# Depthwise taps on TensorE as phases, a modulation on VectorE, and more of a down projection as block products

## The chip, the cores and the metric

The kernel runs on one core of a Trainium2 chip. The metric is the device time of one execution in microseconds (us). The engines are TensorE (PE in the profile), VectorE (DVE), ScalarE (ACT), GpSimd (POOL) and SyncE (SP), whose queue issues most of the DMAs; POOL issues the rest, among them DMAs that add to what lies at their destination.

## The reference

Two layers of a residual trunk on a sequence of 1024 tokens with 1024 channels, all in float32. In both layers:

```
mod = silu(c) @ ada_w[i] + ada_b[i]
sh_m, sc_m, g_m, sh_f, sc_f, g_f = split(mod, 6)          # columns 0 to 5 of the modulation
h = rms_norm(x) * (1 + sc_m) + sh_m
y = conformer_conv(h) in layer 0, multiscale_pool(h) in layer 1
x = x + (1 + g_m) * y
h = rms_norm(x) * (1 + sc_f) + sh_f
x = x + (1 + g_f) * ((silu(h @ w_gate) * (h @ w_up)) @ w_down)      # F = 2816
```

The convolution module of layer 0 is a product to 2048 columns with a gate (GLU), a causal depthwise convolution of width 31 (each channel has 31 taps of its own over the sequence), a layer norm over channels, a silu and a product to 1024. A last RMSNorm ends the stack.

## The kernel before

Channels lie on the 128 partitions, in 8 channel tiles; the sequence is cut into two halves (chunks A and B of 512 tokens). A product in float32 is made of three products of rounded parts: the high part of the weight with the high and with the low part of the activation, and the low part of the weight with the high one (`products`, line 517). So each block of 128 x 128 weights costs three products of 512 columns, and each weight is split into two parts after it has landed, by ScalarE and VectorE (a *direct* weight), or by two passes of ScalarE and a DMA from POOL that adds the weight to its negated high part (a *summed* weight, `load_weight`, line 493).

PE's order is written out by hand: the program is a list of units, each with the weights that it takes, and `run_units` loads the weights ahead in five buffers (`W_BUFS`), with three buffers for raw blocks. The other engines' instructions are ordered by a planner that simulates them. Work of VectorE and POOL that has no fixed place (taps, norms, modulation dots) is kept in tasks, and `pace` lets them step as far as the clocks of a cost model allow (`Engine`, `PRICES`); `finish` forces tasks to their end before the units behind it are written.

Layer 0 starts with the GLU of each channel tile (`conv_in`, `conv_glu`). Two tiles of chunk A get help from PE for their taps: `PE_TAPS = {6: 15, 7: CW}`. A tap on PE is a product with a diagonal block that holds the tap's 128 weights; there are 46 such blocks, in 6 units of up to 8. All other taps are done by VectorE (`ca` in the profile) or by ScalarE and POOL together (`pr` and `pa`), a scaled and shifted add of 512 columns each; the class `Taps` holds them. The order around it: conv of chunk B's tiles 6 and 7 (in one unit with chunk A's), then of tiles 0 and 1, then the units of `pe_taps`, then `finish` of all taps of chunk A, then conv of chunk B's tiles 2, 3 and 4 while chunk A's layer norm (`layer_norm_silu`) runs, then chunk A's product to 1024 (`conv_out`, tile `y`), then tile 5 of chunk B behind which the feed-forward norm of chunk A (`norm_a`) is made.

Columns 2 and 3 of layer 0's modulation, and then 4 and 5, come from PE (`ada_columns`: products of 32 x 256 with c, four side by side, tiles `ada` and `adac`); layer 1's come from VectorE as dots of 1024 columns (`ada_task`).

The feed-forward of layer 0 works on 11 pairs of F tiles. For the pairs from `BEGINS[0] = 8` on, the gate's results are combined over the two halves and the tiles of a pair into seven kinds (`paired` in `joint`), which go to DRAM, and the down projection of those pairs is made of seven block products instead of eight (steps p1 to p7 in `first_down`). The other pairs go the plain way: even tiles of chunk A in `down` between the first heads, odd ones of chunk A in steps a and b, and chunk B's in steps c to f. Each combined step takes a pair of weight tiles and a pair of operand tiles that are split on the way. Chunk A is whole after p4; layer 1's pooling of chunk A (`pool`) then runs beside the rest, and its products (`pool_out`, tile `mx`) stand after step e.

Of the kernel before, what the change touches and what calls it, by code (L numbers as in the profile page):

```python
# [52 lines left out]
PE_TAPS = {6: 15, 7: CW}  # L53
# [7 lines left out]
BEGINS = (8, 0)  # L61
# [38 lines left out]


def tap_groups(p):

    n = PE_TAPS[p]

    todo = list(range(CW - 1, -1, -1) if n == CW else range(CW - 3, CW - 3 - 2 * n, -2))
    return [todo[i : i + DIAGS] for i in range(0, len(todo), DIAGS)]
# [26 lines left out]
def trunk(ctx, tc, xT, c, vec, ada, adan, w1f, w1, wdg, w2, wgu, wdn, wds, wpl, out):  # L134
# [210 lines left out]
    kinds_d = [{q: [dram.tile([P, 2, 2, 512], F32, name=f"kinds_{l}_{q}_{b}") for b in range(3)] for q in BY_SEVEN[l]} for l in range(DEPTH)]  # L345
    KINDS = {"t1": (0, 0), "b22": (0, 1), "t3": (1, 0), "t2": (1, 1), "b11": (2, 0), "t4": (2, 1)}
# [55 lines left out]
    def ada_task(l, js, pause=None, first=None):  # L402

        def gen():
            todo = [(j, k) for j in js for k in range(KT)]
            ws = [ada_load(ada[(l * 6 + j) * KT + k], soft) for j, k in todo[:ADA_BUFS]]
            for i, (j, k) in enumerate(todo):
                yield first if first and i == 0 else pause or ("next" if "pooled" in st else "slow")
                ada_dot(ws.pop(0), l, j, k)
                if i + ADA_BUFS < len(todo):  # L410
                    j2, k2 = todo[i + ADA_BUFS]
                    ws.append(ada_load(ada[(l * 6 + j2) * KT + k2], soft))
# [327 lines left out]
    def conv_glu(ch, p, ba, bg, own=False):  # L740
        u = st["u", ch.i, p]
# [4 lines left out]
        if ch.i == 0 and PE_TAPS.get(p) == CW:  # L746

            V_.scalar_tensor_tensor(ba, ba, V("conv_b1", p), sg, op0=ADD, op1=MUL)
            pair = wpair(B, "us", F32R)
            hi, lo = st["us", p] = [pair[:, i, : ch.width] for i in range(2)]  # L750
            for part in (hi, lo):
                G_.memset(part[:, HALO - 2 : HALO].bitcast(F32), 0.0)
            S_.copy(hi[:, HALO:], ba)
            V_.tensor_tensor(lo[:, HALO:], ba, hi[:, HALO:].bitcast(F32), op=SUB)
            S_.copy(uhalo[:, p, :], ba[:, ch.n - HALO :])
            return
# [6 lines left out]
    def conv_in(*todo, fine=4):  # L763

        def emit(take):
            got = {}
            for each in todo:
# [4 lines left out]
                conv_u(ch, p)  # L772
# [10 lines left out]
                if ch.i == 0 and PE_TAPS.get(p, 0) < CW:  # L783
                    T["taps", 0, p] = Taps(A, p)
                if ch.i == 0 and p == KT - 1:
                    for q in PE_TAPS:
                        if PE_TAPS[q] < CW:
                            split_u(q)
# [3 lines left out]
    def split_u(p):  # L792

        u = st["u", 0, p][:, HALO - 2 : HALO - 2 + A.n]
        hi, lo = st["us", p] = pair("h0", "us")
        S_.copy(hi, u)
        either(A.n).tensor_tensor(lo, u, hi.bitcast(F32), op=SUB)

    def pe_taps(p):


        groups = tap_groups(p)
        us = []
        for i, js in enumerate(groups):
            def emit(take, i=i, js=js):
                if i == 0:
                    st["tap", p] = bank("tap")
                b, wt = st["tap", p], take()
                for q, j in enumerate(js):
                    full = PE_TAPS[p] == CW  # L810
                    o = (CW - 1 - j) // 2 * 2 if full else CW - 3 - j
                    c = j + o if full else 0
                    products(b[:, o:], wt, q, [v[:, c : c + A.n - o] for v in st["us", p]], j == groups[0][0], j == groups[-1][-1])
                    if q % 4 == 3:
                        pace()
                if i == len(groups) - 1:
                    if full:
                        S_.activation(st["u", 0, p][:, HALO:], b, AF.Identity, bias=V("conv_bdw", p))
# [1201 lines left out]
    for p in rest[: len(rest) - HOLD - HOLD_LN]:  # L2020
        conv_in((B, p))
# [235 lines left out]
```

## Time and profile before

| | us |
|---|---|
| median of 3 runs | 1676.87 (1676.09 to 1678.81) |
| profiled execution, its own time | 1675.66 |
| its span from the first to the last instruction | 1673.9 |
| PE busy | 1651.8 |
| VectorE busy | 1310.0 |
| ScalarE busy | 804.1 |
| POOL busy | 487.4 |

An engine is busy while it executes; the span less the busy time is its idle time. The granted TensorE clock was 0.998. The chain of work that ended last, followed back from the last instruction, is 88% products of PE. L128 and L151 are lines of helpers through which all vector instructions and all products are written, so groups are told apart by the tile written and the tiles read (`tap<-us,w`).

### The profile page before, as it was taken

What the parts mean: (1) busy time and instruction counts of PE and PEld (TensorE: products, weight loads), DVE (VectorE), ACT (ScalarE), POOL (GpSimd) and SP (SyncE); (2) the same over time, 40 slices, a digit from 0 to 9 for tenths busy, and PEclk for the clock granted to TensorE, in tenths of its full rate; (3) what the DMA queues carried; (4) which work ended last, traced back from release to release, by engine and by line L of the source; (5) the groups of instructions that cost most, each with busy time, mean ns of one, the idle gap of its engine ahead of it and who ended that gap; (6) DMA issues with size and microseconds to landing.
All of it is one profiled execution on the core that took longest, in us unless ns stands there. A gap on an engine that the chain in (4) does not pass through costs nothing.

```text
span 1673.9 us, 21194 instructions
## 1 busy us (share of the span) xinstructions
PE 1651.8 (99%) x7550; PEld 1351.2 (81%) x7550; DVE 1310.0 (78%) x1867; ACT 804.1 (48%) x1090; POOL 487.4 (29%) x567
## 2 busy tenths in 40 slices
PE   7999999999999999999999999999999999999997
PEld 5777878787888888888888888888888888888887
DVE  8889899799759888888678957848777766658657
ACT  3669696867546332332234436637322222244354
POOL 3587777796002111221100502101111111000013
PEclk9999999999999999999999999999999999999999
DMA  8958997828776888886965959866777776686664
GB/s 301 295 176 228 225 236 205 226 78 241 229 234 168 278 264 287 282 272 206 400 231 164 285 155 283 247 211 199 189 225 222 220 227 183 207 273 207 192 170 126
DMA packets 117180, 378.60 MB, mean 226 GB/s; under 512 B 12369, under 2 KB 14545, under 8 KB 117074
## 3 DMA queue, kind: packets, MB, share of 16 engines
q1 hardware_dynamic: 79664, 245.63, 41.6%
q0 software_dynamic: 36832, 131.09, 32.5%
q8 instruction: 59, 0.97, 0.2%
q10 hardware_dynamic: 578, 0.53, 0.1%
q14 instruction: 47, 0.39, 0.1%
HBM read 310.61 MB, written 62.39 MB: 223 GB/s over the span
## 4 chain that ended last, share of the span: by engine, by line
PE 88%; POOL 3%; DVE 2%; DMA 2%; issue 2%; ACT 2%; DVEq 0%; SPq 0%; POOLq 0%; ACTq 0%
PE a L151 24%; PE dn L151 23%; PE e L151 14%; PE p L151 10%; PE y L151 6%; POOL pa L128 3%; PE first L151 3%; PE g L151 2%; PE tap L151 2%; DMA adaw<-in_adan_dram 1%; DMA s<-in_wds_dram 1%; PE ada L151 1%; ACT w L128 1%; DMA w<-in_wgu_dram 1%; PE var L151 1%
## 5 line engine op out<-in xcount | busy, mean ns | idle before, releaser
L128 ACT CAST w<-raw 128x1024 fp32r<-128x1024 f32 (+1 forms) x247 | 254.6, 1033 | 305.5 <-PE dn L151 56.9
L128 DVE TENSOR_TENSOR w<-raw,w 128x1024 fp32r<-128x1024 f32 (+1 forms) x173 | 209.3, 1214 | 62.2 <-ACT w L128 61.9
L151 PE MATMUL a<-n,w 128*128 128x512 f32 x1056 | 246.8, 389 | 0.2
L151 PE MATMUL p<-h,w 128*128 128x512 f32 x1056 | 243.7, 390 | 1.2 <-DMA w<-in_wgu_dram 1.0
L128 POOL TENSOR_TENSOR pa<-pa,pr 128x512 f32<-128x512 f32 x159 | 225.3, 1500 | 29.0 <-ACT pr L128 23.7
L151 PEld LDWEIGHTS p<-h,w 128*128 128x128 f32 x1056 | 197.3, 188 | 43.7 <-DMA w<-in_wgu_dram 1.4
L151 PEld LDWEIGHTS a<-n,w 128*128 128x128 f32 x1056 | 198.0, 188 | 42.2 <-DVE r L128 1.1
L151 PE MATMUL dn<-hi,w 128*128 128x512 f32 (+1 forms) x768 | 226.2, 377 | 0.4 <-DVE w L128 0.4
L151 PE MATMUL dn<-g,w 128*128 128x512 f32 x864 | 199.1, 390 | 0.2 <-DVE x L128 0.2
L151 PEld LDWEIGHTS dn<-g,w 128*128 128x128 f32 x864 | 161.7, 188 | 34.7 <-DVE x L128 0.6
L128 DVE SCALAR_TENSOR_TENSOR ca<-u,vecs,ca 128x512 f32<-128x512 f32 x246 | 170.6, 747 | 0.5
L151 PEld LDWEIGHTS dn<-hi,w 128*128 128x128 f32 x768 | 141.2, 188 | 27.0 <-DVE w L128 0.9
L151 PE MATMUL dn<-lo,w 128*128 128x512 f32 (+1 forms) x384 | 144.3, 376 | 0.0
L151 PE MATMUL a<-t,w 128*128 128x512 f32 x528 | 123.3, 389 | 0.0
L151 PE MATMUL e<-t,w 128*128 128x512 f32 x528 | 123.3, 389 | 0.0
L151 PE MATMUL e<-b,w 128*128 128x512 f32 x528 | 123.3, 389 | 0.0
L128 ACT ACTIVATE pr<-u,vecs 128x512 f32<-128x512 f32 x159 | 108.4, 717 | 25.0 <-POOL pa L128 19.7
L151 PEld LDWEIGHTS a<-t,w 128*128 128x128 f32 x528 | 99.1, 188 | 20.7
L151 PEld LDWEIGHTS e<-t,w 128*128 128x128 f32 x528 | 99.1, 188 | 20.6
L151 PEld LDWEIGHTS e<-b,w 128*128 128x128 f32 x528 | 99.1, 188 | 20.6
L1191 POOL DMA_DIRECT2D raw<-in_wgu_dram x41 | 36.5, 889 | 271.5 <-DVE r L128 104.2
L128 ACT CAST hi<-op 128x1024 fp32r<-128x1024 f32 (+1 forms) x52 | 48.5, 935 | 87.1 <-PE dn L151 77.2
(191 smaller groups left out, 2449.4 us busy)
## 6 DMA issues: line engine op xcount, KB each, us to landing
raw<-in_wgu_dram SPq DMA_DIRECT2D x132, 512.0 KB, 4.7
raw<-in_wds_dram SPq DMA_DIRECT2D x48, 512.0 KB, 6.0
adaw<-in_ada_dram POOLq DMA_DIRECT2D x48, 512.0 KB, 6.8
kinds<-k POOLq DMA_DIRECT2D x42, 512.0 KB, 7.7
raw<-in_wgu_dram POOLq DMA_DIRECT2D x41, 512.0 KB, 7.3
raw<-in_w_dram SPq DMA_DIRECT2D x36, 512.0 KB, 6.6
op<-kinds SPq DMA_DIRECT2D x36, 512.0 KB, 4.8
adaw<-in_adan_dram SPq DMA_DIRECT2D x32, 512.0 KB, 5.5
```

The source lines that it names most:

```text
L128: self.last = self.order(getattr(self.eng, name)(out, *args, **kw))
L151: last_mm[0] = nc.tensor.matmul(out, lhsT, rhs, start=start, stop=stop, skip_group_check=more).ins.name
L1191: d = order(nc.gpsimd.dma_start(w[i], wgu[l, fp, src], accum_op=ADD))
```

## The change

Three parts.

**Taps of channel tiles 6 and 7.** All 31 taps of both tiles go to PE, for both chunks. After the GLU the values of a tile are written to DRAM by phases (token modulo 4) and read back with 32 channels x 4 phases on the partitions, for each of four groups of 32 channels. Along the partitions a product then sums over four neighbouring tokens, and nine blocks of weights, each shifted by one column of four tokens, hold all taps. For each tile, 4 groups x 9 blocks, with three products of 256 columns each (both chunks at once), in 9 units of 8 blocks; every other one of these weights is direct. ScalarE copies the results out, they go to DRAM and come back by channels, and ScalarE adds the bias into `u` (`tapped`). The units of taps now stand behind the conv of chunk B's tile 0, and its tile 1 behind them. Chunk B's tiles 6 and 7 have no taps left on the other engines, nor has chunk A's tile 6.

**Columns 4 and 5 of layer 0's modulation** come from VectorE as dots, with loads on SP's queue.

**Layer 0's down projection**: `BEGINS[0]` is 6 instead of 8, so pairs 6 to 10 (F tiles 12 to 21) are made by seven block products. The even tiles of pairs 6 and 7 keep only half of their plain products for chunk A between the heads; p2 leaves pairs 6 and 7 out. Steps a and b have three units instead of four, the steps of chunk B run over three quads of tiles, the blocks a22 are loaded where they are used, four low parts of one quad's operands are made by POOL, and the pooled products stand after step d.

```diff
-PE_TAPS = {6: 15, 7: CW}
+ON_PE = (6, 7)
+PHASES = 4
+GC = P // PHASES
+NM = (CW - 1 + 2 * (PHASES - 1)) // PHASES
+LEAD = NM - 1
+SEG = 2 * WSLOT // PHASES
...
-BEGINS = (8, 0)
+BEGINS = (6, 0)
...
+    def phased(ch, p, ba, sg):
+        n = ch.n // PHASES
+        t = temp(ch.n, "ny", 2)
+        V_.scalar_tensor_tensor(t.rearrange("p (f n) -> p f n", f=PHASES), ba.rearrange("p (n f) -> p f n", f=PHASES), V("conv_b1", p),
+                                sg.rearrange("p (n f) -> p f n", f=PHASES), op0=ADD, op1=MUL)
+        d = phased_d[p][ch.i]
+        sync.dma_start(d.rearrange("p f n -> p (f n)"), t)
+        if ch.i == 0:
+            st["us", p] = phase_parts(p)
+        o = LEAD + ch.i * n
+        view = d.rearrange("(g c) f n -> f c g n", c=GC)
+        for gs, hi, lo in st["us", p]:
+            for f in range(PHASES):
+                sync.dma_start(lo[GC * f : GC * f + GC, : len(gs), o : o + n].bitcast(F32), view[f][:, gs[0] : gs[-1] + 1])
+            at = (slice(None), slice(0, len(gs)), slice(o, o + n))
+            S_.copy(hi[at], lo[at].bitcast(F32))
+            V_.tensor_tensor(lo[at], lo[at].bitcast(F32), hi[at].bitcast(F32), op=SUB)
...
+    def pe_taps():
+        blocks = [(p, g, m) for p in ON_PE for g in range(PHASES) for m in range(NM)]
+        n = S // PHASES
...
+                    products(b[:, g % 2 * n : g % 2 * n + n], wt, q, (hi, lo), m == 0, m == NM - 1, more=True)
...
+                    if m == NM - 1 and g % 2:
+                        out_ = temp(2 * n, "acc", 2)
+                        S_.copy(out_, b)
+                        sync.dma_start(tapped_d[p][:, g - 1 : g + 1], out_.rearrange("p (g n) -> p g n", g=2))
+                        if g == PHASES - 1:
+                            tapped(A, p)
...
+        for i in range(0, len(blocks), DIAGS):
+            units_.append((emit_of(blocks[i : i + DIAGS]), wdg[i // DIAGS] if i // DIAGS % 2 else direct(wdg[i // DIAGS])))
...
+    def tapped(ch, p):
...
+        t = temp(ch.n, "ny", 2).rearrange("p (f n) -> p f n", f=PHASES)
+        view = tapped_d[p].rearrange("(f c) g n -> g c f n", f=PHASES)
+        for g in range(PHASES):
+            sync.dma_start(t[GC * g : GC * g + GC], view[g][:, :, ch.i * n : ch.i * n + n])
+        S_.activation(u[:, HALO:].rearrange("p (n f) -> p n f", f=PHASES), t.rearrange("p f n -> p n f"), AF.Identity, bias=V("conv_bdw", p))
+        st["taps", ch.i][p] = True
...
-                gs = [st["g", ch.i, f] for f in fs]
+                gs = [st["g", ch.i, f] for f in fs if not d0 or f // 2 < BEGINS[l]]
...
-            V_.tensor_tensor(lo[:, :w], raw[:, :w], hi[:, :w].bitcast(F32), op=SUB)
+            eng = G_ if not l and q == 3 and kind in ("b11", "t2", "t3", "t4") else V_
+            eng.tensor_tensor(lo[:, :w], raw[:, :w], hi[:, :w].bitcast(F32), op=SUB)
...
+            at_once = {"a12": 1, "s4": 1, "a22": 3, "s2": 3}.get(kind)
+            if at_once is not None:
+                mine["a22" if kind == "s2" else kind] = r = raws.tile([P, D], F32, tag="raw", name=nm("raw"))[:, :n]
+                nc.sync.dma_start(r, wds[l, q, at_once][:, :n])
...
+            mine = [q for q in qs if kind != "a12" or q >= ROUNDS[l] * ROUND // 2]
...
-        classical(A, range(duo), 0, ("odd",), "a")
-        classical(A, range(duo), 1, ("odd",), "b")
+        classical(A, range(begins), 0, ("odd",), "a")
+        classical(A, range(begins), 1, ("odd",), "b")
...
-        for qs, names in ((range(duo // 2), "cd"), (range(duo // 2, duo), "ef")):
+        for some_qs, names in ((range(2), "cd"), (range(2, begins), "ef")):
...
-    for p in rest[: len(rest) - HOLD - HOLD_LN]:
+    first, *others = rest[: len(rest) - HOLD - HOLD_LN]
+    conv_in((B, first))
+    for u in pe_taps():
+        unit(*u)
+    for p in others:
         conv_in((B, p))
-    for p in PE_TAPS:
-        for u in pe_taps(p):
-            unit(*u)
+    unit(lambda take: [tapped(B, p) for p in ON_PE])
...
-        T["ada_f"] = Task(ada_columns((4, 5)), False, 0)
-        T["ada_f"].free = True
+        T["ada_f"] = ada_task(0, (4, 5), queue=sync)
     unit(ada_second)
-    taps(B, *some, *rest[: len(rest) - HOLD - HOLD_LN])
+    taps(B, *rest[: len(rest) - HOLD - HOLD_LN])
...
-        "e": lambda: pool_end(A),
+        "d": lambda: pool_end(A),
```

More of the change, by code (lines that the diff above doesn't have):

```diff
@@ L745, in conv_glu @@
             tc.add_manual_dep(S_.last.ins, st.pop("v_high"), edge, reason="behind the layer norm's last high part")
[L746 to L755, printed above, removed]
+        if p in ON_PE:
+            phased(ch, p, ba, sg)
             return
@@ L799, in pe_taps, with phase_parts @@
[L799 to L813, printed above, removed]
+    def phase_parts(p):
+        if p == ON_PE[0]:
+            hi, lo = (wpair(B, "us", F32R).rearrange("p a (b w) -> p (a b) w", w=SEG) for _ in range(2))
+            parts = [(range(PHASES), hi, lo)]
+        else:
+            parts = [(range(o, o + 2), block("h0", "us"), block("h0", "us")) for o in range(0, PHASES, 2)]
+        for _, hi, lo in parts:
+            for part in (hi, lo):
+                G_.memset(part[:, :, :LEAD].bitcast(F32), 0.0)
+        return parts
@@ new lines, in pe_taps, with emit_of, emit @@
+    def pe_taps():
+        blocks = [(p, g, m) for p in ON_PE for g in range(PHASES) for m in range(NM)]
+        n = S // PHASES
+        units_ = []
+        def emit_of(these):
+            def emit(take):
+                wt = take()
+                for q, (p, g, m) in enumerate(these):
+                    if m == 0 and g % 2 == 0:
+                        st["tap"] = bank("tap")
+                    b = st["tap"]
+                    hi, lo = next((hi[:, g - gs[0], m : m + n], lo[:, g - gs[0], m : m + n]) for gs, hi, lo in st["us", p] if g in gs)
+                    products(b[:, g % 2 * n : g % 2 * n + n], wt, q, (hi, lo), m == 0, m == NM - 1, more=True)
@@ L832, in __init__ @@
             self.ch, self.p, self.done, self.urgent = ch, p, False, False
-            self.acc, self.part, self.other = None, None, None
-            others = tap_groups(p) if ch.i == 0 and p in PE_TAPS else []
-            self.todo, self.awaits = [j for j in range(CW - 1) if not any(j in js for js in others)], bool(others)
+            self.acc, self.part = None, None
+            self.todo = list(range(CW - 1))
             tasks.append(self)
@@ L1655, in first_down @@
         SIDE = {"odd": 0, "even": 1}
-        duo, one = BY_SEVEN[l]
-        todo, raw, banks, ready, counts = [], {duo: {}, one: {}}, {}, {}, [0, 0]
+        qs = list(BY_SEVEN[l])[::-1]
+        begins = BEGINS[l] // 2
+        raw, banks, ready, counts = {q: {} for q in qs}, {}, {}, [0, 0]
         steps = []
```

114 lines of the change are left out of this document (47 added, 67 removed).

## The prediction

> **What bounds the kernel now.** I read the first two parts of the page, then who made TensorE (PE) wait, then the busy time by stage.
>
> ```profile
> span 1673.9 us, 21194 instructions
> PE 1651.8 (99%) x7550; PEld 1351.2 (81%) x7550; DVE 1310.0 (78%) x1867; ACT 804.1 (48%) x1090; POOL 487.4 (29%) x567
> PE   7999999999999999999999999999999999999997
> ...
> PE p L151 <- DMA w<-in_wgu_dram: 1.0, 1, 1.0
> ...
> 66.00:167.00 101.00, 100.71 (x523) 75.21 (x522) 91.50 (x144) 83.18 (x121) 79.49 (x75) 1.00 0.75 215
> 167.00:200.00 33.00, 33.00 (x159) 26.67 (x152) 31.05 (x48) 22.80 (x30) 29.16 (x27) 1.00 0.89 220
> 200.00:245.00 45.00, 44.95 (x236) 34.77 (x235) 38.01 (x64) 37.18 (x50) 27.76 (x27) 1.00 0.95 240
> ...
> 816.00:860.00 44.00, 44.00 (x196) 36.44 (x195) 24.60 (x34) 9.71 (x12) 3.79 (x7) 1.00 0.93 350
> 860.00:918.00 58.00, 58.00 (x264) 48.17 (x263) 51.20 (x73) 26.69 (x35) 3.30 (x12) 1.00 0.52 153
> ```
>
> A window row gives its length and then the busy time of PE, weight loads, VectorE (DVE), ScalarE (ACT) and POOL; its last numbers are clock, DMA share and GB/s. The 22.1 us that PE is idle lie almost all in the first and the last slice. Between them its longest wait is 1.0 us, and in the stages that the change touches (167 to 245 us, 816 to 918 us) it has next to none. So the order of products written for PE sets the time: a product taken out is worth its issue time, unless one of the others, which must now deliver sooner, comes too late.
>
> **The price of a product.** A product's "mean ns" overlaps its neighbours, so I take the time of runs in the chain of waits (start, length, what).
>
> ```profile
> 167.38 5.69 PE tap L151 x24
> 173.64 7.68 PE tap L151 x33
> 181.66 18.47 PE tap L151 x81
> ...
> 516.73 5.44 PE e L151 x24
> ...
> 1650.24 6.47 PE dn L151 x54
> ...
> L151 PE MATMUL dn<-hi,w 128*128 128x256 f32 x36 | 6.7, 285 | 0.0
> L151 PEld LDWEIGHTS dn<-hi,w 128*128 128x128 f32 x35 | 5.5, 191 | 0.0
> ```
>
> 512 columns: 5.44 / 24 = 0.227 us. 256 columns, as in the last stage: 6.47 / 54 = 0.120 us, each with a weight load of its own (the last two rows, window 1650.3 to 1656.7 us). I take 0.120.
>
> **Taps.** Removed: 15 taps of tile 6 and 31 of tile 7, three products each, 138; they take 5.69 + 7.68 + 18.47 = 31.8 us. Added: 2 tiles x 4 output groups x 9 blocks x 3 products of 256 columns = 216, for both halves of the sequence: 216 x 0.120 = 25.9 us. PE: **-5.9 us**. If the short products ran at half the 512 price, 0.114, it would be -7.2; if each took the 0.191 of its weight load, +9.5. VectorE and POOL lose 62 taps of the second half and 16 of the first, and two closing sums.
>
> The Trainium skill (TensorE: Matmul & The Clock Gate, Part 3, "What overlaps and what doesn't") says that weight loads overlap running matmuls only where their row groups differ; all of these use the whole array, so by it each load would stand in series. By that rule the change would lose at this place; the row above (0.120 us with a 191 ns load) goes against it, and I give it a small chance below.
>
> **Modulation.** Columns 4 and 5 of the modulation leave PE:
>
> ```profile
> 211.84 1.07 PE L151 MATMUL ada<-adaw,ccols 128*32 128x256 f32 x16
> 212.84 5.78 PE L151 MATMUL a<-h,w 128*128 128x512 f32 x24
> ...
> 267.91 0.50 PE L151 MATMUL adac<-quarters,t 128*128 128x4 f32 x4
> 268.27 11.13 PE L151 MATMUL y<-v,w 128*128 128x512 f32 x48
> ...
> 317.56 1.07 PE L151 MATMUL ada<-adaw,ccols 128*32 128x256 f32 x16
> ...
> 921.02 1.22 DVE L128 SCALAR_TENSOR_TENSOR adaw<-adaw,cact 128x1024 f32<-128x1024 f32 x1
> ```
>
> Eight such pairs stand between the first row and the last of its kind, 1.00 us each (212.84 - 211.84), and two turns of 0.36 (268.27 - 267.91): **-8.7 us**. VectorE gets 16 dots of 1.22 us, 19.5 us over some 100 us, less than half of the 62 taps that it and POOL no longer do (0.66 us each on VectorE, 9.30 / 14 in the row under step 2: 41 us); the same 512 KB per dot is loaded on the same queue (SP). The dots are paced 6 us apart; column 4 needs eight, 48 us, and comes before the 336 products ahead of it (76 us) have passed, so its forced finish costs nothing. If that cover were gone, each dot left over would be 1.2 us of wait for the feed-forward norm.
>
> **Down.** Pairs 6 and 7 took 2 x 96 = 192 products in the plain form (2 tiles x 2 halves x 8 x 3 a pair) and take 2 x 84 = 168 as seven blocks: 24 fewer of 0.227, **-5.4 us**. Their kind sums replace splits of the same size on VectorE, under joint units for which PE waited nowhere.
>
> Together -20.0 us on PE. Now what is late next.
>
> **1. The feed of the tap weights.** A unit is 24 products, 24 x 0.120 = 2.9 us, where it was 5.7.
>
> ```profile
> raw<-in_wdg_dram SPq DMA_DIRECT2D x6, 512.0 KB, 6.9
> w<-in_wdg_dram POOLq DMA_DIRECT2D x6, 512.0 KB, 9.3
> ...
> L128 ACT CAST w<-raw 128x1024 fp32r<-128x1024 f32 (+1 forms) x247 | 254.6, 1033 | 305.5 <-PE dn L151 56.9
> L128 DVE TENSOR_TENSOR w<-raw,w 128x1024 fp32r<-128x1024 f32 (+1 forms) x173 | 209.3, 1214 | 62.2 <-ACT w L128 61.9
> L506 POOL DMA_DIRECT2D w<-in_wdg_dram x6 | 7.0, 1165 | 4.3 <-ACT t L128 2.8 <-ACT w L128 1.6
> ```
>
> Five weight buffers: a buffer freed by one unit is needed four units later, 11.5 us. A summed weight takes two ACT passes (2.1), the issue (1.2) and 9.3 us of landing, 12.6 us; a direct one, with its raw block already there, 1.0 + 1.2 = 2.2 us. Four of nine are summed, and two of those fill a buffer inside the run: 2 x 1.1, I take **+2 us**. Bounds: nothing, if the landing is the 6.9 of the other queue; +7 if SP is held up once by a pair of the new writes (rival b). SP carries eight writes to DRAM here, with reads that wait at the head of the queue until they have landed, and the raw weights queue behind those. The nearest write-and-read-back is that of the kind sums:
>
> ```profile
> kinds<-k POOLq DMA_DIRECT2D x42, 512.0 KB, 7.7
> op<-kinds SPq DMA_DIRECT2D x36, 512.0 KB, 4.8
> ```
>
> The way there and back is 7.7 + 4.8 = 12.5 us. Between the last product of tile 6's second half and its first tap product lie 96 others (21.8 us: tile 7 and one conv tile more); tile 7's have 48 and the 108 tap products of tile 6 (10.9 + 13.0 = 23.9 us). Both cover the way, by 9 us.
>
> **2. Layer norm of the first half.** All its taps must be in before its mean.
>
> ```profile
> 170.75 9.30 DVE L128 SCALAR_TENSOR_TENSOR ca<-u,vecs,ca 128x512 f32<-128x512 f32 x14
> ...
> 203.35 1.50 DVE L128 TENSOR_TENSOR acc<-acc,u 128x512 f32<-128x512 f32 x2
> 205.43 1.02 PE L151 MATMUL mean<-acc,ones 128*128 128x512 f32 x2
> 221.41 6.01 DVE L128 SCALAR_TENSOR_TENSOR ca<-u,vecs,ca 128x512 f32<-128x512 f32 x9
> ...
> 238.91 11.58 PE L151 MATMUL y<-v,w 128*128 128x512 f32 x48
> ...
> 241.92 0.69 DVE L128 TENSOR_TENSOR v<-t,v 128x512 fp32r<-128x512 f32 x1 [1.11 <-ACT v L128]
> ...
> L128 DVE SCALAR_TENSOR_TENSOR ca<-u,vecs,ca 128x512 f32<-128x512 f32 x118 | 81.9, 748 | 0.4
> L128 POOL TENSOR_TENSOR pa<-pa,pr 128x512 f32<-128x512 f32 x65 | 92.6, 1566 | 8.0 <-ACT pr L128 4.2 <-ACT uhalo L128 3.1
> ```
>
> The sum is ready at 204.85 and the mean runs at 205.43: 0.6 us of room. PE will be there 5.9 us sooner. By the last two rows (window 66 to 205.5 us) VectorE did about 63% of the taps. So 16 taps and their closing give back some 8.7 us on VectorE and 8.4 on POOL, and two fewer summed weights 2.3 on POOL. Five direct tap weights (5 x 1.2) and two more splits take 7 us of VectorE. What is left, 1.7 us of VectorE (0.66 a tap) and 10.7 of POOL (92.6 / 65 = 1.42 a tap), is 10.1 taps; both engines together do 2.22 taps in a us, so the sum is ready 4.5 us sooner: 0.8 us late. From mean to y three modulation pairs fall out (3.0 us); the last low part ends at 242.6 and is read at 238.91 + 7 x 0.68 = 243.7, 1.1 us of room: 1.9 us late. Together **+2.7 us**. Bounds: 0, if the fillers between its steps move aside (6 us of other taps stand there); 8.8 if nothing of it gets sooner. The path from the last tap product through ACT, DRAM and ACT again (one cast, 12.5 us by the rows, one scatter) ends near 195, some 14 us behind the last product, ahead of the vector taps.
>
> **3. First down.** The classical part ahead of the blocks (a, b) shrinks from 8 units to 6, 43.5 to 32.6 us, and "d" takes the place of "e" as the point where the pooling must be done:
>
> ```profile
> 964.30 0.68 DVE L128 TENSOR_TENSOR mx<-win,mx 128x512 fp32r<-128x512 f32 x1
> ...
> 983.47 11.04 PE L151 MATMUL y<-mx,w 128*128 128x512 f32 x48
> ```
>
> It ends at 965.0 for products at 983.5, 18.5 us of room. From the end of p4 to these products there were 72 products of p5 and p3 (16.3 us) and 288 of c, d, e (65.3); there will be 120 (27.2) and 192 (43.5), 10.9 us less, which leaves 7.6. VectorE had 51.2 of 58 us busy in the old blocks, but a step of two pairs is 5.4 us of products for 2.4 of splits, and four splits go to POOL, which had 3.3. The loads are nearer: 350 GB/s over 44 us is 15.4 MB; less two weights (1.0 MB) it takes 41 us in a window of 33, 8 us late if all of it were wanted by the first block. Most is not, so I take **+1.5 us**, between 0 and 8.
>
> **Sum.** 1675.7 (the profiled execution, 1673.9 of span and 1.8 around it) - 20.0 + 2 + 2.7 + 1.5 = 1661.9. The median of the runs is 1.2 us above that execution: **1663 us**, 0.8% faster.
>
> **Rivals.** (a) *The waits eat half.* Layer norm and first down take their upper bounds, 8.8 + 8, in place of 4.2: 1676 us, within 0.2%; with one of them 1669. For it: the 0.6 and 1.1 us of room. Against it: VectorE and POOL lose 78 taps. (b) *SP's queue becomes the bound, and it is slower.* The writes come in pairs (two output copies of a tile, two halves of its values). If both hold the head of SP for 7.7 us, 15.4 us stand against the three raw blocks loaded ahead, 3 x 2.9 = 8.7: PE waits 6.7 us. Four pairs make 26.8: 1676.9 - 20.0 + 26.8 = 1684 us. It is slower than before once a hold costs over 6.9 us (2 x 6.9 - 8.7 = 5.0, four times 20). For it: the DMA share of 0.89 to 0.95 there. Against it: a write is 256 KB, not 512, and the first two pairs fall under conv products, where a weight lasts 5.4 us and not 2.9. (c) *Weight loads don't hide* behind 256 columns: 216 x (0.191 + 0.120) = 67.2 us, +35.4 on the old taps: 1676.9 + 35.4 - 14.1 = 1698. Against it stands the 0.120. (d) *Nothing is late*: 1657.
>
> **How the numbers follow.** Forecast 0.58, (d) 0.12, (a) 0.17 (a third of it near 1676), (b) 0.10, (c) 0.03. A change under 0.2% (3.4 us) can't be told from none. Faster: 0.58 + 0.12 + 0.11 = 0.81; within 0.2%: 0.06 of (a) and 0.01 of (b), 0.07; slower 0.12. The range runs from 1655 (d with 0.114 us a product) to 1677, the far end of (a); (b) and (c) lie outside.
>
> **What would show it.** Right: 216 tap products at 0.12 us in about 26 us; no modulation products after the taps; 24 fewer down products; PE busy near 1632 us and its idle time 22 + 6. Wrong: PE waiting in the taps for weights over 4 us (step 1), for the mean or y over 5 (step 2), in p2 to p6 or ahead of the pooled y (step 3). A rate of 0.15 us or more would upset the first term; a wait of PE for the tap values themselves, the cover of the round trip.

## The result and the profile after

The changed kernel takes 1736.12 us (median, 1732.8 to 1739.1) where the kernel before, on the same chip, takes 1677.62: a ratio of 1.0349, 95% interval 1.0328 to 1.037. It is 3.5% slower; the forecast was 1663 us, and no rival reached this far. The profiled execution took 1736.28. One execution of an experiment below (2063.7 us, at a granted clock of 0.75) fell in a slower state of the chip and is left out of that experiment's median.

The first lines of the page of the kernel after:

```profile
span 1734.4 us, 21107 instructions
PE 1650.5 (95%) x7468; PEld 1353.3 (78%) x7468; DVE 1330.2 (77%) x1848; ACT 804.3 (46%) x1086; POOL 491.5 (28%) x556
...
PEclk9999999799999999999999999999999999999999
```

PE is idle for 83.9 us (1734.4 - 1650.5) where it was 22.1. And it is busy for as long as before, though 20 us of products are gone: the clock row has a dip, and products are slower there. The span's growth is then -20.0 (products) + 61.8 (idle) + 18.7 (what is left of busy time: 1650.5 - 1651.8 + 20.0) = 60.5 us. By stage, the first answer is the kernel before, the second the kernel after (columns as in the prediction, where the first row of the kernel before stands, 66 to 167 us). The stages are: up to the first tap product; to the first product of the feed-forward; to `y` of the second half; to the blocks of the first down; to the pooled `y`; the rest.

```profile
167.00:300.00 133.00, 132.95 (x677) 105.17 (x670) 120.72 (x194) 99.31 (x135) 100.31 (x90) 1.00 0.87 223
300.00:450.00 150.00, 148.49 (x680) 119.84 (x679) 133.78 (x189) 109.62 (x161) 95.67 (x74) 1.00 0.61 181
450.00:860.00 410.00, 409.89 (x1815) 339.19 (x1814) 316.85 (x437) 146.69 (x194) 68.95 (x112) 1.00 0.84 270
860.00:984.00 124.00, 124.00 (x555) 102.83 (x554) 101.08 (x146) 54.07 (x69) 25.81 (x48) 1.00 0.69 209
984.00:1674.00 690.00, 681.10 (x3103) 566.88 (x3101) 489.53 (x671) 284.46 (x380) 93.02 (x124) 1.00 0.70 208
```

```profile
66.00:155.00 89.00, 88.18 (x454) 66.22 (x452) 79.99 (x119) 72.01 (x107) 65.77 (x60) 1.00 0.74 212
155.00:326.00 171.00, 138.54 (x721) 115.74 (x719) 133.08 (x201) 115.56 (x158) 112.34 (x98) 0.90 0.79 209
326.00:497.00 171.00, 148.91 (x617) 119.00 (x618) 138.72 (x184) 107.40 (x155) 93.37 (x69) 0.93 0.63 195
497.00:896.00 399.00, 398.89 (x1767) 330.08 (x1766) 310.23 (x429) 137.97 (x180) 68.17 (x111) 1.00 0.82 262
896.00:1044.00 148.00, 140.34 (x605) 113.93 (x604) 122.56 (x160) 60.27 (x75) 38.80 (x52) 0.98 0.63 198
1044.00:1734.00 690.00, 681.35 (x3102) 566.94 (x3101) 489.15 (x669) 284.75 (x380) 88.91 (x121) 0.99 0.68 206
```

The first stage is 12 us shorter, and the fourth and fifth trade some 11, only because units stand elsewhere in PE's order (48 conv products behind the first tap, 48 down products behind the first block). The loss lies in three stages: 38 us, less those 12, around the taps and the first norms, 21 up to the second half's `y`, and 24, less those 11, in the blocks. The last 690 us are the same to the microsecond. The five largest waits of PE after (in total, times, longest):

```profile
PE mean L148 <- DVE acc L125: 21.8, 2, 12.4
PE p L148 <- ACT h L125: 15.1, 1, 15.1
PE p L148 <- ACT r L125: 8.2, 2, 7.1
PE var L148 <- DVE acc L125: 8.1, 2, 6.0
PE dn L148 <- DVE x L125: 4.3, 4, 2.1
```

**Place 1, the mean of the first half (12.4 us).** PE's rows, then ScalarE's, then those of SP's queue (in brackets the idle time before a row and what ended it; L148 and L125 are the helpers' lines here that were L151 and L128 before):

```profile
160.04 8.60 PE L148 MATMUL tap<-us,w 128*128 128x256 f32 x47 [3.91 <-DMA raw<-in_wdg_dram]
...
169.14 5.99 PE L148 MATMUL tap<-us,w 128*128 128x256 f32 x48
...
189.70 1.67 PE L148 MATMUL tap<-us,w 128*128 128x256 f32 x12
...
220.12 2.05 PE L148 MATMUL mean<-acc,ones 128*128 128x512 f32 x2 [12.37 <-DVE acc L125]
```

```profile
194.58 0.56 ACT L125 COPY acc<-tap 128x512 f32<-128x512 f32 x1
...
210.81 1.17 ACT L125 ACTIVATE u<-ny,vecs 128x512 f32<-128x512 f32 x1 [10.63 <-DMA ny<-tapped]
211.88 0.67 ACT L125 ACTIVATE t<-g,vecs 128x512 f32<-128x512 f32 x1
...
218.08 2.26 ACT L125 ACTIVATE u<-ny,vecs 128x512 f32<-128x512 f32 x2
```

```profile
196.24 0.43 SPq L166 DMA_DIRECT2D tapped<-acc  x1
196.72 1.97 SPq L166 DMA_DIRECT2D ny<-tapped  x4
201.99 2.55 SPq L495 DMA_DIRECT2D raw<-in_w_dram  x2
209.28 4.45 SPq L166 DMA_DIRECT2D ny<-tapped  x6
```

```profile
SPq L166 <- DMA tapped<-acc: 13.2, 4, 4.7
```

The last tap product ends at 191.4, its result is copied at 194.6, written to DRAM from 196.2, read from 209.3 on and scattered at 218.1: 27 us where the prediction had 14. The last row (of SP's waits) shows SP at the head of its queue for that write, which landed at 209.2, 13.0 us after its issue. Meanwhile ScalarE stands 10.6 us at a scatter whose values have not come. It is not the one that the mean needs: it belongs to the second half's tile 6, whose four reads went out at 196.7, while the first half's last two went out only at 209.3. Behind it in ScalarE's queue stands the sigmoid of the next conv tile (`t<-g`), for which VectorE then waits 10.1 us; VectorE's own sums end at 218.1, the one with the scattered values at 220.0.

**Place 2, the feed-forward norm (15.1 us).** PE, then VectorE:

```profile
325.81 0.80 PE L148 MATMUL p<-h,w 128*128 128x512 f32 x1 [15.13 <-ACT h L125]
```

```profile
304.56 2.21 DVE L125 SCALAR_TENSOR_TENSOR adaw<-adaw,cact 128x1024 f32<-128x1024 f32 x1
...
322.07 1.23 DVE L125 SCALAR_TENSOR_TENSOR adaw<-adaw,cact 128x1024 f32<-128x1024 f32 x1 [2.45 <-DMA adaw<-in_ada_dram]
...
324.25 1.40 DVE L125 SCALAR_TENSOR_TENSOR t<-x,gains,rstd 128x512 f32<-128x512 f32 x2 [0.94 <-POOL gains L125]
```

Six dots run between the norm's root (done at 304.6) and the first value of the norm, which needs column 4 from them. They were not late: `mean_rsqrt` puts the last six dots (`recent`, `RECENT = 6`) behind the root, so that they don't delay it. Here the norm itself wants the column. Their loads run only two ahead, so three of the six also waited for a load, 9.1 us together.

**Place 3** is the second half's layer norm (9.4 us ahead of its mean, 7.1 behind it), **place 4** the blocks of the first down. The 6.0 us ahead of a `var` are none of the change's places: they lie at 11.9 us, where the kernel before waits 4.9.

### The profile page after: what moved, and what is told of

Its sections match the earlier page's. It is cut to its first block, busy times and chain, and to the rows that moved or that the text cites. A ratio compares the mean times of both kernels' runs of the same rounds, so it can differ in the third digit from the quotient of the medians.

```text
span 1734.4 us, 21107 instructions
## 1 busy us (share of the span) xinstructions
PE 1650.5 (95%) x7468; PEld 1353.3 (78%) x7468; DVE 1330.2 (77%) x1848; ACT 804.3 (46%) x1086; POOL 491.5 (28%) x556
## 5 line engine op out<-in xcount | busy, mean ns | idle before, releaser
L125 ACT CAST w<-raw 128x1024 fp32r<-128x1024 f32 (+1 forms) x242 | 250.0, 1036 | 282.1 <-DMA raw<-in_wgu_dram 56.6
L148 PE MATMUL p<-h,w 128*128 128x512 f32 x1056 | 251.2, 398 | 24.2 <-ACT h L125 15.1
L148 PE MATMUL dn<-hi,w 128*128 128x512 f32 (+1 forms) x864 | 259.4, 381 | 6.1 <-DVE x L125 4.0
L148 PEld LDWEIGHTS p<-h,w 128*128 128x128 f32 x1056 | 202.4, 193 | 69.1 <-ACT h L125 15.5
L125 DVE TENSOR_TENSOR w<-raw,w 128x1024 fp32r<-128x1024 f32 (+1 forms) x172 | 217.3, 1268 | 41.4 <-ACT w L125 41.3
L148 PE MATMUL a<-n,w 128*128 128x512 f32 x1056 | 246.8, 389 | 0.2
L148 PEld LDWEIGHTS a<-n,w 128*128 128x128 f32 x1056 | 198.1, 188 | 42.1 <-DVE r L125 1.1
L125 POOL TENSOR_TENSOR pa<-pa,pr 128x512 f32<-128x512 f32 x148 | 218.8, 1528 | 41.4 <-ACT pr L125 38.0
L148 PEld LDWEIGHTS dn<-hi,w 128*128 128x128 f32 x864 | 160.8, 190 | 39.5 <-DVE x L125 3.4
L148 PE MATMUL dn<-g,w 128*128 128x512 f32 x696 | 161.3, 391 | 3.5 <-DVE g L125 2.5
L148 PE MATMUL dn<-lo,w 128*128 128x512 f32 (+1 forms) x432 | 164.4, 381 | 0.0
L148 PEld LDWEIGHTS dn<-g,w 128*128 128x128 f32 x696 | 130.0, 188 | 32.9 <-DVE g L125 3.7
L125 DVE SCALAR_TENSOR_TENSOR ca<-u,vecs,ca 128x512 f32<-128x512 f32 x188 | 130.3, 746 | 0.2
L148 PE MATMUL a<-t,w 128*128 128x512 f32 x528 | 123.3, 389 | 0.0
L148 PE MATMUL e<-t,w 128*128 128x512 f32 x528 | 123.2, 389 | 0.0
L148 PE MATMUL e<-b,w 128*128 128x512 f32 x528 | 123.2, 389 | 0.0
L148 PEld LDWEIGHTS a<-t,w 128*128 128x128 f32 x528 | 99.1, 188 | 20.7
L148 PEld LDWEIGHTS e<-t,w 128*128 128x128 f32 x528 | 99.1, 188 | 20.6
L148 PEld LDWEIGHTS e<-b,w 128*128 128x128 f32 x528 | 99.1, 188 | 20.6
L125 DVE SCALAR_TENSOR_TENSOR adaw<-adaw,cact 128x1024 f32<-128x1024 f32 x80 | 104.8, 1315 | 10.3 <-DMA adaw<-in_ada_dram 10.3
L125 ACT ACTIVATE pr<-u,vecs 128x512 f32<-128x512 f32 x148 | 100.9, 716 | 22.9 <-POOL pa L125 15.4
```

The lines of the kernel that those rows point to most:

```text
L125: self.last = self.order(getattr(self.eng, name)(out, *args, **kw))
L148: last_mm[0] = nc.tensor.matmul(out, lhsT, rhs, start=start, stop=stop, skip_group_check=more).ins.name
```

## The experiments

The time of the kernel before in these comparisons was 1676.5 to 1677.6 us. "Offset" is how much later than before a point in PE's row comes.

### Each part alone

The diff is cut into its three parts and each is put alone on the kernel before.

> The kernel before with the first part alone (taps of tiles 6 and 7 as phases). Theory 1 (each part brings a wait of its own; here the way of the tap results back through DRAM, 27 us from the last tap product to the vector sum instead of the 14 that was reckoned): a wait of PE for the first layer norm's mean of 8 to 14 us, products at a lower granted clock behind it, 1685 to 1700 us. Rival (the three parts only hurt together, because they share the DMA queues and VectorE): no wait over 3 us, about 1672 us.

> The kernel before with the second part alone (columns 4 and 5 of the first layer's modulation as dots on VectorE). Theory 1 (six dots of column 4 are ordered behind the root of the very norm that needs them, by the list of the last six dots that the norm puts behind its root): six dots between the root and the first scaled value, a wait of PE for h of 10 to 16 us at the first heads, 1680 to 1695 us. Rival (dots are only late because the taps' transfers hold up their loads): column 4 done before the root, about 1669 us.

> The kernel before with the third part alone (five pairs by seven block products). Theory 1: some 7 to 8 us of idle time of PE between the first block products and the pooling, 1676 to 1684 us. Rival (its waits come from the stages ahead of it): no idle time there, 1672 us.

Measured: taps 1692.73 us (ratio 1.0089, 1.0072 to 1.0106), modulation 1712.42 (1.021, 1.0195 to 1.0226), down 1697.59 (1.0118, 1.0103 to 1.0133). Each part alone is slower. +15.7, +35.4 and +20.6 make 71.7, more than the 58.5 of the whole, so they share some waits. The taps fit their expectation; the other two cost 17 and 14 us more than the upper ends given.

### The held dots

```diff
-        task.dots = True
+        task.dots = l > 0
```

> The changed kernel, but the dots of the first layer's modulation are not put on the list of the last six dots, so nothing orders them behind the norm's root. Theory 1: the wait for h at the first heads falls from 15.1 to under 3 us and its lower clock goes with it: 1710 to 1718 us. Rival (the dots are late because their loads or the cost model's pace hold them up): the wait stays above 10 us, 1732 to 1740 us.

1725.6 (1.029, 1.0275 to 1.0305): the wait for `h` is gone, 10.5 of its 15.1 us are gained, and the second half's mean waits 11.7 us instead of 9.4. The hold is shown as the cause of that wait. Part of what it cost is handed on.

### The way back of the taps

First, the reads of the first half written 13 us of products after the write, the scatter 9 us after those (`tapped` as a task with two pauses, `LOAD` giving their lengths):

```diff
+        def gen():
+            if not ch.i:
+                yield "written"
...
                 sync.dma_start(t[GC * g : GC * g + GC], view[g][:, :, ch.i * n : ch.i * n + n])
+            yield "read"
...
+        Task(gen(), False, 0).free = True
```

> The taps alone, with their way back written as three steps: the write to DRAM, the reads 13 us of products later, the scatter and the mark 'done' 9 us after that; the mean of the first half so moves 36 products (8 us) back in PE's order, and no engine stands with a read that is not there yet. Theory 'the return trip is late and blocks SP, ACT and VectorE': the wait of 12.9 us ahead of the mean falls to under 3, the time falls from 1692.7 to 1674-1681. Rival 'VectorE's own taps are what is late (the return is only the last to be named)': the mean still waits 4-8 us, 1684-1692. Rival 'moving the mean back uncovers y': y waits on v for 4 us or more, 1684-1692.

1706.58: 14 us worse than the taps alone. The mean's place in PE's order moved by 8 us, and its last values came later still: the scatter that it waits for is at 225.4, the mean at 227.3 instead of 220.3. The first half's `y` now waits 6.8 us too. The round trip itself is late, and putting its steps off only adds to it. Then three places mended at once, the two edits above and, in `layer_norm_silu`:

```diff
+        if ch.i:
+            yield "held"
         yield "soon" if ch.i else "stats"
         b = bank("mean")
```

> The whole change with three places mended: the return trip in three steps (as in the run before), the dots of columns 4 and 5 no longer held behind the norm's root, and the second half's mean put 14 us of products later in PE's order (72 products more ahead of it, 72 fewer between it and its y). Theory 'these three places carry what is lost ahead of the joint part': the waits for h (15.1), both means (12.4, 9.5) and var (6.0) go, with some 8-15 us of halved clock behind them; 1736.1 - 43 - 10 = 1683, between 1676 and 1694, what is left over the forecast of 1663 being the first down and the y of the second half. Rival 'VectorE has too much to do between the first mean and the second half's y, with the dots': the waits only move to y and v, 1700-1722.

1711.22 (1.0198, 1.0183 to 1.0213): 25 us gained, 17 above the range; the waits for `h` and the second mean are gone, the first mean still waits 12.2 us, and the first half's `y` 7.8, as the rival had it. Then the first half's gather left out (the scatter reads the copied bank):

```diff
-                            tapped(A, p)
+                            tapped(A, p, out_)
```

> The taps alone, but the first half's values of tiles 6 and 7 are scattered straight from the copy of the last tap bank (not the right ones: the gather from DRAM for that half is left out; the second half's stays). Theory 'the way back through DRAM, in queues that are full, and the engines that stand behind it are what is late': the wait of 12.9 us ahead of the first mean falls under 3, VectorE's gap of 10 us ahead of it goes, and the time falls from 1692.7 to 1672-1682. Rival 'VectorE's taps of the other six tiles are late by themselves': the mean still waits 5 us or more, 1685-1693.

1692.72: no gain at all, although the first mean now waits 1.8 us. ScalarE, then PE, of this run:

```profile
219.22 1.23 ACT L125 ACTIVATE u<-ny,vecs 128x512 f32<-128x512 f32 x1 [9.72 <-DMA raw<-in_w_dram]
220.36 0.57 ACT L125 COPY ny<-mean 128x512 f32<-128x512 f32 x1
```

```profile
208.73 1.10 PE L148 MATMUL mean<-acc,ones 128*128 128x512 f32 x2 [1.77 <-DVE acc L125]
...
229.89 1.87 PE L148 MATMUL var<-ones,acc 128*128 128x1 f32 x8 [7.90 <-DVE acc L125]
```

The scatter of the *second* half, which nobody needs for another 180 us, stands in ScalarE's queue ahead of the copy of the first half's mean. It holds the norm until 219, and the wait turns up at `var`. (The releaser that the row names is a weight's raw block; the instruction reads `ny`.) So the second half's gather was put 50 us later, its scatter 12 us behind it, and then the first half's left out as well:

```diff
+            if ch.i:
+                yield "home"
             for g in range(PHASES):
                 sync.dma_start(t[GC * g : GC * g + GC], view[g][:, :, ch.i * n : ch.i * n + n])
```

> The taps alone, the second half's gather and scatter 50 us of products later (they are wanted only for the second layer norm, 180 us later). Theory 'the engines stand behind the second half's values too': ScalarE has no gap of 9 us behind the first mean, the wait ahead of var (5.3 us) goes, the first half's own way back stays (mean waits 8-12 us); 1692.7 falls to 1680-1687. Rival 'VectorE is late by itself': 1689-1695.

> As the run before, and the first half's gather is left out again (its values of tiles 6 and 7 are not the right ones). If the two gathers are the whole loss, no wait for mean, var or y over 2 us, only the 4 us ahead of the first tap product are left: 1677 - 5.9 + 4 to 6 = 1674-1678. If VectorE's order is the rest: 1683 or more.

1695.57 (1.0109, 1.0088 to 1.013) with the first half's gather alone, above both ranges given (the first mean waits 15.8 us), 1681.91 (1.0024, 1.0015 to 1.0034) with neither. Both gathers: 1692.7; only the second half's: 1692.7; only the first half's: 1695.6; none: 1681.9. Either of them holds the same queues as long as both; together, not singly, they are 10.8 us. Of the 10.2 us left over the forecast for this part (1681.9 against 1677.6 - 5.9), its trace shows 4.0 of wait ahead of the second tap product, 1.8 ahead of the mean, 1.3 of slower products behind the first wait (47 in 7.20 us, where 48 take 5.99 later) and 1.0 in the rate of the taps: 8.1 in an execution (1679.6) that was 2.3 below the median.

### The modulation

The part alone with the dots not held (the edit of `task.dots`), then with the dots replaced too:

```diff
-                ada_dot(ws.pop(0), l, j, k)
+                (ada_dot if l else ada_none)(ws.pop(0), l, j, k)
...
+        V_.tensor_copy(mod[:, b : b + 1], w[:, :1])
```

> The modulation alone, with its dots no longer held behind the norm's root. Theory 'the hold is what costs': the wait for h (12.4 us) goes and the time falls from 1712.4 to 1690-1698. Rival 'VectorE is short of time up to the second layer norm': the wait for h goes, but the waits for the second half's acc and v grow by most of it, 1702-1712.

> As the run before, and the sixteen dots are left out (each a copy of one column; the loads, the gains and the order of products of PE stay as the planner then makes them), so columns 4 and 5 are wrong. Theory 'the 19.5 us of dots on VectorE are the rest of the loss, since VectorE is the engine that the second layer norm waits for': 1666-1673, the 8.7 us of products taken out being all that is left. Rival 'the loads on SP or the gains on POOL cost it': 1685 or more.

Not held: 1709.57, 2.8 less than with the hold. Dots left out too: 1689.61. So the hold explains little of this part alone; the dots cost 20.0 us for 19.5 us of VectorE's time, one for one. VectorE has none to give there. Its busy time is the fifth number (after PE and the weight loads) in the windows of the run with dots, not held:

```profile
390.00:420.00 30.00, 30.00 (x129) 24.71 (x128) 29.93 (x35) 24.54 (x38) 29.33 (x24) 0.96 0.87 235
420.00:450.00 30.00, 21.37 (x83) 16.00 (x82) 29.27 (x35) 12.91 (x20) 24.56 (x16) 0.94 0.38 128
```

And with no dots it is still 13 us slower than before, with 8.7 us of products *taken out*. The time lies where the rival had it (1685 or more), but its causes don't show: from 205 to 450 us there are 14 loads of 512 KB for the modulation on SP, as many as before, and the gains take 0.9 us of POOL for 0.8. Neither was left out by itself. VectorE and POOL in that run:

```profile
393.05 11.00 DVE L128 TENSOR_TENSOR g<-ny,g 128x512 fp32r<-128x512 f32 x1
```

```profile
392.90 13.68 POOL L128 TENSOR_TENSOR pa<-pa,pr 128x512 f32<-128x512 f32 x10
```

A VectorE operation of 0.68 us took 11.0 beside ten POOL additions without a gap. To see whether that is the loss, POOL's additions were made to wait for the VectorE instruction written ahead of them:

```diff
                     G_.tensor_tensor(self.part, self.part, pr, op=ADD)
+                    if ch.i:
+                        tc.add_manual_dep(G_.last.ins, V_.last.ins.name, held_by, reason="in step with VectorE")
```

> The modulation without dots and hold (1689.6), and each POOL addition of the second half's taps waits for the VectorE instruction that the planner wrote ahead of it, so that POOL can no longer run ten of them without a gap. Theory 'POOL's back-to-back additions keep VectorE's two-operand instruction out': no VectorE operation of 128x512 over 2.2 us between 300 and 450 us, PE's waits for r (6.1) and mean (5.1) go, 1672-1681. Rival 'the order of products is what is worse': the stretched operation is gone and the time stays above 1686.

1691.4 (1.0079, 1.0058 to 1.0099): no gain. The longest VectorE operation from 300 to 450 us is now 5.3 us (3.1 where the 11.0 stood), but POOL ends its additions later (18 of them from 395 to 424) and the mean waits 9.9 us. What the two engines lose to each other was moved, not removed; that this stretching is the whole 13 us is not shown.

### The down projection

The four low parts on VectorE again, and a tenth pair of heads ahead of the second half's `y`, first singly, then together:

```diff
-            eng = G_ if not l and q == 3 and kind in ("b11", "t2", "t3", "t4") else V_
+            eng = V_
...
-HEADS = (9, 8)
+HEADS = (10, 8)
```

> The down part alone, with the four low parts of pairs 6 and 7 on VectorE again instead of POOL. Theory 'a low part on POOL stretches the VectorE operation beside it (1.22 to 3.4 us), and the update of x that a bank waits for stands behind it': no VectorE operation of 128x1024 over 1.5 us, PE's waits for x fall from 6.0 to about 3, the time from 1697.6 to 1690-1695. Rival 'VectorE simply has too much work in the blocks': its work grows by 4.9 us less 4.4 of stretching, 1697-1702.

> The down part alone, with a tenth pair's heads for the first half ahead of the second half's y (48 products, 11 us, moved there from behind it; the same products in all). Theory 'the 24 down products that went out of the heads were cover of the second layer norm': the three waits of y on v (7.9 us) and the halved clock behind them go, 1697.6 - 8 to -12 = 1685-1690, and what is left over the 1671.5 that the products alone give (14-18 us) is lost in the blocks. Rival 'the loss sits in the blocks and the earlier lateness is only passed on': 1694-1699.

> The down part with low parts on VectorE and a tenth pair's heads ahead of the second half's y. If the two causes add up: 1690.1 - 8 to -12 = 1678-1683. Rival 'what the tenth pair saves at y is given back in the joint part and ahead of the pooled norm', as it was with the low parts on POOL: 1687-1694.

1690.06 (1.0079, 1.0064 to 1.0094), 1700.48 (1.0135, 1.012 to 1.015) and 1692.24 (1.0092, 1.0071 to 1.0111). The groups of the blocks (850 to 1000 us) in the down part alone, then with the low parts on VectorE:

```profile
L128 DVE TENSOR_TENSOR s<-a,raw 128x1024 f32<-128x1024 f32 x2 | 4.6, 2310 | 0.0
...
L128 POOL TENSOR_TENSOR lo<-op,hi 128x1024 fp32r<-128x1024 f32 x4 | 13.4, 3360 | 48.4 <-ACT hi L128 48.4
```

```profile
L128 DVE TENSOR_TENSOR s<-a,raw 128x1024 f32<-128x1024 f32 x2 | 2.4, 1220 | 0.0
```

Four low parts moved back to a VectorE that was full gain 7.5 us: the sums beside them fall from 2.31 to 1.22 us, and the low parts themselves from 3.36 to 1.22 (the run doesn't part the two). In the blocks up to the pooled `y` the stage loses 4 us instead of 14. The tenth pair takes all waits away ahead of the second half's `y` (7.9 us), the first joint product comes 11.9 us sooner (511.4 for 523.3), and the end is 2.2 us later in these executions (2.9 in the medians): 7.8 are given back in the joint part, the rest in layer 1 behind the pooled `y`, where a `var` waits 5.5 us. The rival was right, with both causes taken away too.

### All named causes at once

The edits above on the whole change: `task.dots`, `yield "held"`, `tapped(A, p, out_)` and `eng = V_`.

> The whole change with every cause named so far taken away: no gather for the first half's taps (values not the right ones), dots not held, the second half's mean 14 us later in PE's order, low parts of pairs 6 and 7 on VectorE. If these are all: 1736.1 goes to 1668-1682, of which 1663 was the forecast and the rest the 4 us wait ahead of the first tap product and the waits that are left in the blocks. If it stays above 1690, something else takes part, and the stage where the offset to the kernel before grows names it.

1696.04 (1.0112, 1.0093 to 1.0131): 40 of the 73 us between the change and its forecast are taken back, and it stays 14 us over the range given. The second half's gather was left in here (`var` waits 6.5 us at 227.7): the offset to the kernel before is 4 at the first mean and 12 at the first feed-forward product. In the blocks it grows by 15, 11 of them by the moved products.

### What a product is worth, and where

The same 28 products (the high weight with the low value) left out of the kernel *before*, once ahead of the second half's mean, once in the last joint part; nothing added, nothing moved:

```diff
+            if i == 1 and st.get("less"):
+                st["less"] -= 1
+                clock["PE"] += 512 / 2400 + 0.0025
+                continue
```

> The kernel before with 28 products left out of its first heads (the product of the high weight with the low value in 28 steps, at 300 to 320 us), the order of all else kept: 28 x 0.227 = 6.4 us less on PE, nothing added or moved. Theory 'up to the second half's y, VectorE and POOL end as late as PE, so products are worth nothing there': PE waits for the second mean or for y some 6 us longer, and the time stays within 1674-1679 (with halved clock behind the wait it may even be a little slower). Rival 'PE sets the time there, as its 22 us of idle time say': 1670.5.

> The control: the same 28 products left out of the last joint part (near 1300 us) of the kernel before. Where PE alone sets the time a product is worth its issue time: 1677 - 6.4 = 1670.5, between 1669.5 and 1672. If it gains nothing here either, the worth of a product was wrong as such, not its place.

1679.02 in the heads (1.0016, 1.0006 to 1.0026: nothing gained), 1671.50 in the joint part (0.9967, 0.9954 to 0.998: 5.2 us of 6.4). PE in the heads of the former:

```profile
319.04 4.62 PE L151 MATMUL p<-h,w 128*128 128x512 f32 x12 [3.20 <-ACT ny L128]
324.64 0.61 PE L151 MATMUL adac<-quarters,t 128*128 128x4 f32 x4 [0.98 <-ACT t L128]
```

PE is 6.4 us early and gives it back within 11 us: 3.2 in a wait for ScalarE, 1.9 in twelve products that take 4.62 us instead of 2.72, 1.0 in another wait. The expectation had the place wrong (the mean), not the worth. At the second mean the kernel before has no more room either (VectorE, then PE):

```profile
415.83 0.69 DVE L128 TENSOR_TENSOR acc<-acc,u 128x512 f32<-128x512 f32 x1
```

```profile
416.66 1.10 PE L151 MATMUL mean<-acc,ones 128*128 128x512 f32 x2
```

The sum is done at 416.5, the mean runs at 416.7, right behind the product ahead of it.

## Why the prediction was wrong

**"So the order of products written for PE sets the time: a product taken out is worth its issue time."** This step failed first. It holds in the last joint part (5.2 of 6.4 us), and not in the heads (0 of 6.4), though PE never waits there. The sentence goes on "unless one of the others, which must now deliver sooner, comes too late", but the stages read for that end at 245 us and begin again at 816; the heads and the second half's norm lie between. A wait of zero was read as "the others are early"; it also stands where they come just in time. The windows had it: VectorE busy 31.05 of 33 us and 38.01 of 45 in the prediction's rows, 133.78 of 150 in the row of the heads above. The heads are where the modulation's dots ran, and their lead-in is the first norms' taps, so the -8.7 could hardly be had in full (argued from this place, not measured at those products), and the dots, put on VectorE alone, cost their time one for one. Whether the taps' -5.9 would have stood by itself is not shown; with both gathers gone, 10 us of other waits and rates still hide it.

**Taps, the price of a product**: 5.99 / 48 = 0.125 us against 0.120 forecast, 27 for the 216. Right; rival (c) is refuted.

**Step 1, the feed of the weights**: 3.9 us of wait ahead of the taps for +2, within its bounds, but by luck: it is no wait for a weight. The second product takes the same high part of the weight as the first, and the low part of the values, which VectorE writes last (first row, of the kernel after: done at 159.99, the product runs at 160.04). The second row, of the taps alone, names it; the row of place 1 names a weight's raw block instead.

```profile
158.76 1.23 DVE L125 TENSOR_TENSOR us<-us,us 128x512 fp32r<-128x512 f32 x1
```

```profile
160.96 7.31 PE L148 MATMUL tap<-us,w 128*128 128x256 f32 x47 [3.44 <-DVE us L125]
```

What failed is "Both cover the way, by 9 us". Write and reads took 9.9 us (143.9 to 153.7), less than the 12.5 reckoned. But the last product of tile 6's second half ended at 130.3, its GLU came only at 142.7, and the split stood 4.3 us in VectorE's queue: 29.7 us in all, against a cover of 25.5. No row shows the taps waiting for a weight.

**Step 2, "the path from the last tap product ... ends near 195, some 14 us behind the last product"**: the step that failed for the taps. It ended at 219, 28 us behind. The sum took the landing times of two other transfers (7.7 + 4.8) as if the copy, the queue and the scatter came free. In this stage the copy stood 3.2 us in ScalarE's queue, the write landed after 13.0 us, the last read after 5.4 (at 214.6), and the scatter stood another 3.4 us in ScalarE's queue. What was not asked at all: what stands *behind* an instruction that waits for a DMA. On ScalarE it was the next tile's sigmoid and, without the first half's gather, the copy of the first mean, both behind a scatter of the second half. Step 2's bound (8.8) was worked out from VectorE's taps alone. The cover that was worked out, on the way *in*, fell short by the 3.9 of step 1.

**Modulation, "its forced finish costs nothing"**: the stated price of lost cover, 1.2 us a dot, would have made 7.2 for six dots. The wait was 15.1, since the dots were held on purpose, by a rule in `mean_rsqrt` that the prediction had not looked up, and three of them then waited for a load. With the hold gone this part still cost 33 us: the dots' own 20.0, one for one, which the prediction had set against the 62 taps taken off (41 us). Those belong to another part; alone, the modulation has no such relief. What the dots cost in the whole change was not measured.

**Down**: "under joint units for which PE waited nowhere" was right (399 us after, of 410 less 10.9). Two terms were missed. The 24 products came out of the cover of the second layer norm, which step 3 didn't look at (7.9 us of waits; alone, the first joint product came at 523.3 instead of 516.6, where it should have come 5.4 sooner). And "four splits go to POOL, which had 3.3" counted POOL's time and not what it does to VectorE's. Pooling itself, the wait that step 3 was about, did not come up.

**Rivals.** (a), the waits eat half, had the kind right and a fifth of the size. (b) had SP held up by the writes right (13.2 us in four waits for the tap results) and the price wrong: it put it on the tap weights. (d), nothing is late, is refuted with the forecast. The forecast's sum of lateness was 6.2 us; it is 79 (1736.1 - 1676.9 + 20.0). Left open: some 13 us of the modulation without dots, and what keeps the kernel with all named causes but the second half's gather taken away 20 us above the kernel before.

## What to carry to other kernels

An engine that never waits is not thereby the only bound: before a product is priced as a gain, look up how close behind the others end, at every point where they meet (0.1 us at the second mean), and how full they are in that stage. When a value comes by DMA, list what stands behind its consumer in that engine's queue, and give a round trip the landing times of its own stage, its queue included. In a schedule balanced to a microsecond, one long wait is paid twice: in the wait and in the slow products after it.

## What the runs showed of the hardware

**VectorE held up by POOL.** An operation with two operands in SBUF took 2.31 us beside POOL's low parts and 1.22 without, and 11.0 instead of 0.68 beside ten additions of POOL. The Trainium skill (SBUF — State Buffer, "Who interferes with whom") has the rule: such an operation and a POOL instruction that reads SBUF exclude each other, and whichever comes second waits until the first is done. The trace agrees on who blocks. But the 11.0 us are some seven additions of 1.37, not one: VectorE didn't get its turn between them. VectorE's taps, whose running sum `ca` lies in PSUM and not in SBUF, kept their 0.67 us beside such additions (ten in 6.67 us from 386.8 us on, in the last run of the modulation).

**The clock after a wait.** Windows of the kernel after (the third number from the end is the granted clock):

```profile
311.00:326.00 15.00, 0.20 (x1) 0.20 (x1) 6.93 (x11) 1.37 (x3) 1.03 (x4) 0.57 0.71 213
326.00:331.00 5.00, 4.09 (x9) 2.90 (x10) 5.00 (x9) 2.06 (x4) 0.00 (x0) 0.50 0.35 115
```

Nine products took 4.09 us there, 0.45 each, twice the 0.227 of the prediction. The Trainium skill (TensorE: Matmul & The Clock Gate, Part 1, "What's actually happening") has the clock halve after an idle window of about 3.4 us. Shorter waits did it here: with 28 products out of the heads, after 3.20 us, twelve products took 0.385 us each, and in the down part alone, after waits of 2.03 and 0.56 us close together, seventeen fitted into 7 us at a clock of 0.51:

```profile
879.92 0.47 PE L151 MATMUL dn<-hi,w 128*128 128x512 f32 x1 [2.03 <-DVE x L128]
...
883.54 0.79 PE L151 MATMUL dn<-hi,w 128*128 128x512 f32 x1 [0.56 <-DVE x L128]
```

```profile
881.00:888.00 7.00, 6.44 (x17) 4.53 (x16) 7.00 (x10) 5.32 (x8) 0.00 (x0) 0.51 0.62 207
```

After 1.48 us, in the same run, it stayed at 1.00. The length of the wait alone doesn't decide it: in the whole change with the dots not held it stayed at 1.00 after 2.31 us (the window from 400 to 406 us). The prediction had no term for this, and the 18.7 us by which PE's busy time exceeds its products I find no other cause for in the rows but 1.0 in the rate of the taps.
